# Products of a zero tile on TensorE ahead of and between the first transposes of a hybrid encoder layer

## The chip, the cores and the metric

The kernel runs on one core of a Trainium2 chip. The metric is the device time of one execution in microseconds, taken as the median of several runs. A core has five engines with queues of their own: TensorE (PE, its weight loads PEld), VectorE (DVE), ScalarE (ACT), GpSimd (POOL) and SyncE (SP), which here issues nearly all DMA transfers. Each engine takes its instructions in the order in which they stand; semaphores tie the engines together.

## The reference

One layer of an encoder over 1024 tokens of width 1024, all in float32, with a norm ahead of and behind each part:

```
h = rms_norm(x, g_mix_pre)
aq, ak, av, dqkv, dgate, dalpha, dbeta = split(h @ w_in)
attn_o = window_attention(rope(aq), rope(ak), av, sink)          # 8 heads, +-128 tokens
dn_o   = gated_deltanet(dqkv, dgate, dalpha, dbeta, conv_w, ...) # 4 heads, both directions
x = x + rms_norm(concat(attn_o, dn_o) @ w_out, g_mix_post)
x = x + rms_norm(cross_attention(rms_norm(x), rms_norm(mem)), g_cross_post)  # 256 memory tokens
f = (silu(gate) * up) @ w_down                                   # gate, up = h' @ w_gate_up, 2816 wide each
x = x + rms_norm(f, g_ffn_post)
```

The change concerns only the first line, `h = rms_norm(x, g_mix_pre)`, and the first projections of it.

## The kernel before

The kernel is one long program for one core. Every float32 matrix product is made of three products of a shorter float type: each operand is split into a rounded part (`hi`, a cast on ScalarE, line 103) and what is left (`lo`, a subtraction on VectorE or GpSimd, line 104), and hi·hi, lo·hi and hi·lo are summed in PSUM (`gemm_b`, line 276).

The program has these stages: the norm of x and its transposition; the projections, with convolutions and the chunked products of the DeltaNet (to about 350 us); the scan over eight chunks in both directions, interleaved with the windowed attention and the projections of the memory (to about 545 us); then the output projection, cross-attention and the feed-forward part, in a form with fewer products.

At the start, x is loaded as eight token tiles `xt` of 128 x 1024, in two halves of four (lines 211 to 216). With them come `grow`, the gain as rows, and `ident`, the identity for transpositions. For each half, ScalarE sums the squares of a token tile (line 230) and takes a root (168), VectorE inverts it (169) and scales the tile in place (233). TensorE then transposes 128 x 128 pieces of the four tiles (239), four pieces to a PSUM tile `ps`, of which there are five. ScalarE casts such a tile times the gain to `hhi` (241), VectorE cuts the rest to `hlo` (242). The first projections (276) use them as they come:

```
for k in range(KT):
    pt = small()
    for j in range(4):
        nc.tensor.transpose(pt[:, j * P:(j + 1) * P], xts[4 * hf + j][:, k * P:(k + 1) * P], ident)
    g = gcol[:, k:k + 1]
    cast = nc.scalar.activation(hi[:, k, :], pt, AF.Identity, scale=g)
    cut = nc.vector.scalar_tensor_tensor(lo[:, k, :], pt, g, f32(hi[:, k, :]), ALU.mult, ALU.subtract)
```

The order on each engine isn't the order of the code. A scheduler places the instructions by its own timeline of the whole program, with raised priority for weight loads and some orders pinned by `issue_after`. So an instruction that is added at the start can change what stands where further on.

The names of the scan that the prediction uses: `kv` holds a chunk's keys, values and queries, `psc` are the scan's PSUM tiles (line 843); VectorE corrects `kv` (871) before TensorE can go on. In the attention, `sc` are scores and probabilities, scaled by VectorE at line 703; `ptw` their transposes (711), `ph` and `pl` their split, and `pow` their products with the values (716). The weights of the memory's keys are split by ScalarE (`whi`) and GpSimd (`wlo`). The DeltaNet's products of keys and queries, in float32 without a split, are at line 474.

The pool `wt` has one buffer under the tag `A`, which is used next for `abT` near 47 us; the pool `pg` has three PSUM tiles of 512 columns, used in turn by the projections.

Of the kernel before, what the change touches and what calls it, by code (L numbers as in the profile page):

```python
# [10 lines left out]
F32 = mybir.dt.float32  # L11
# [8 lines left out]
P = 128  # L20
# [56 lines left out]
def tile_hybrid_block(  # L77
# [6 lines left out]
    nc = tc.nc  # L84
# [4 lines left out]
    if dump is None:  # L89
        def dump(name, ap):  # L90
            pass


    def f32(ap):
        return ap.bitcast(F32)
# [12 lines left out]
    def pool(name, bufs, **kw):  # L108
        return tc.tile_pool(name=name, bufs=bufs, reuse_waits="tile", **kw)
# [41 lines left out]
    wt = p1.enter_context(pool("wt", 1, side="right"))  # L151
# [15 lines left out]
    def inverse_root(rs, ss, scale, bias):  # L167
        root = nc.scalar.activation(rs, ss, AF.Sqrt, bias=bias, scale=scale)
        nc.vector.reciprocal(rs, rs)
        return root  # L170
# [27 lines left out]
    pg = pgs.enter_context(pool("pg", 3, space=PSUM))  # L198
# [5 lines left out]
    def small():  # L204
        return ps.tile([P, 512], F32, tag="ps", name="ps")


    xts = [t1.tile([P, D], F32, tag="xt", name="xt", bufs=NT) for _ in range(NT)]
# [3 lines left out]
    for t in range(NT):  # L212
        xload.append(nc.sync.dma_start(xts[t], x[t * P:(t + 1) * P, :]))
        if t == 0:
            nc.sync.dma_start(grow, g_mix_pre[0].rearrange("(c p) -> c p", p=P))
            nc.sync.dma_start(ident, consts[:, 0:P])
    warm = t1.tile([P, 1], F32, tag="ss", name="warm", bufs=4)
    nc.scalar.activation(warm, epsc, AF.Sqrt)
    pt = small()
# [3 lines left out]
    for hf in range(2):  # L223
        hi = hx.tile([P, KT, HALF], F32R, name=f"hhi{hf}")
        lo = hx.tile([P, KT, HALF], F32R, name=f"hlo{hf}")
        for j in range(4):
            xt = xts[4 * hf + j]
            junk = t1.tile([P, D], F32, tag="junk", name="junk", bufs=1)
            ss = t1.tile([P, 1], F32, tag="ss", name="ss", bufs=4)
            nc.scalar.activation(junk, xt, AF.Square, accum_out=ss)  # L230
            rs = t1.tile([P, 1], F32, tag="rs", name="rs", bufs=4)
            rooted = inverse_root(rs, ss, 1.0 / D, epsc)
            scaled = nc.vector.tensor_scalar(xt, xt, rs, None, ALU.mult)
        if hf == 0:
            ready.append((rooted, scaled))
# [6 lines that stand above are left out]
            cut = nc.vector.scalar_tensor_tensor(lo[:, k, :], pt, g, f32(hi[:, k, :]), ALU.mult, ALU.subtract)  # L242
            if hf == 0 and k == 5:
                ready.append((cast, cut))
        hT.append((hi, lo))
        dump(f"hT{hf}", (hi, lo))

# [82 lines left out]
    for hf in range(2):  # L330
        pp = pg.tile([P, 512], F32, tag="pg", name="pg")
        for k in range(KT):
            for a in range(2):
                nc.tensor.matmul(pp, wabr[:, k, :], hT[hf][a][:, k, :], start=(k == 0 and a == 0),
                                 stop=(k == KT - 1 and a == 1))
# [693 lines left out]
    pg = p3.enter_context(pool("pg3", 4, space=PSUM))  # L1029
# [335 lines left out]
    def four(spec):  # L1365
        return [p_.tile([P, HALF], F32, tag=t_, name="pst") for p_, t_ in spec]
# [8 lines left out]
    A = four([PG] * 4)  # L1375
# [155 lines left out]
    for e in range(EARLY):  # L1531
        f = 2 * e
        w, A = [], []
# [84 lines left out]
    pg = L0.enter_context(pool("pg4", 8, space=PSUM))  # L1618

    def bank(name):  # L1620
        return pg.tile([P, 512], F32, tag="pg", name=name)

    for f in (2 * p for p in turns):
# [10 lines left out]
        for i, (W1, W22, (S1, S2, S3, S4), *_) in enumerate(wts):  # L1634
            a1, v, u = (tg.tile([P, 512], F32, tag=n, name=n, bufs=b_) for n, b_ in (("a1", 1), ("v", 2), ("u", 1)))
            A = None
            if early:
                nc.sync.dma_start(a1, d_m1[f + i])
            else:
                A = bank("pA")  # L1640
# [10 lines left out]
        for i, (W1, W22, (S1, S2, S3, S4), *_) in enumerate(wts):  # L1651
            A, D_, E_, v = st[i]
# [105 lines left out]
    A = [bank("pdA") for _ in range(4)]  # L1758
# [118 lines left out]
```

## Time and profile before

| | |
|---|---|
| median of 3 runs | 1521.06 us (1518.25 to 1524.97) |
| profiled execution | 1518.84 us, its span 1516.8 us |
| TensorE busy | 1471.5 us, 97% of the span |
| VectorE, ScalarE, GpSimd busy | 1101.3, 784.2, 362.8 us |
| DMA | 256.34 MB, mean 169 GB/s |

In the profile a row of the order of time has the start and the length in us, then the engine, the line of the code, the operation, the tile written and the tiles read, sizes, and a count where like instructions are merged. Brackets hold the idle time of the engine just before, and what ended it. A row of windows has for each engine the busy time and the number of instructions, and behind these the granted clock of TensorE as a share of full speed, the DMA's busy share and GB/s. Matmuls are pipelined, so that the length of one is longer than the step from one to the next.

### The profile page before, as it was taken

To read this page: it belongs to the slowest core of one execution; us is meant where nothing else is said; L and a number is where in the kernel's file an instruction comes from. 1 tells how busy PE (TensorE), PEld (TensorE's weight loads), DVE (VectorE), ACT (ScalarE), POOL (GpSimd) and SP (SyncE) were. 2 spreads that over 40 slices of the span, in tenths; PEclk is the share of its full clock that TensorE was granted. 3 is DMA by queue.
4 is the path that set the end of the run, shared out by engine and by line. 5 is a ranking of instruction groups with operands and counts; after the bars stand their busy time and mean duration, and the time that the engine had idled before them with its cause. 6 is when DMAs were issued, how large, how long until landed. Compare 5 with 4: busy or idle time off the path is not lost.

```text
span 1516.8 us, 21323 instructions
## 1 busy us (share of the span) xinstructions
PE 1471.5 (97%) x7437; PEld 1239.2 (82%) x7437; DVE 1101.3 (73%) x1801; ACT 784.2 (52%) x1606; POOL 362.8 (24%) x394
## 2 busy tenths in 40 slices
PE   7999999998999999999999998999999999999998
PEld 6888877888989878887788876888888888888787
DVE  5878998676998775538466867776867764696666
ACT  7678844567556764555454684332332332453533
POOL 0011232432325303342201002433524342000030
PEclk9999999999999999999999999999999999999999
DMA  6245554557987584448625553334434333853255
GB/s 203 70 118 142 148 164 129 157 171 193 345 283 234 180 293 158 162 151 262 232 90 180 194 190 123 118 119 132 132 112 152 126 103 116 323 207 97 105 179 168
DMA packets 257751, 256.34 MB, mean 169 GB/s; under 512 B 18128, under 2 KB 190317, under 8 KB 257645
## 3 DMA queue, kind: packets, MB, share of 16 engines
q1 hardware_dynamic: 256493, 252.90, 52.3%
q10 hardware_dynamic: 1152, 2.10, 0.4%
q8 instruction: 58, 0.95, 0.3%
q14 instruction: 48, 0.39, 0.1%
HBM read 178.63 MB, written 73.70 MB: 166 GB/s over the span
## 4 chain that ended last, share of the span: by engine, by line
PE 64%; DVE 8%; DMA 5%; ACT 2%; issue 2%; POOL 1%; SPq 0%; DVEq 0%; ACTq 0%; POOLq 0%
PE pE L1514 8%; PE pD L1514 8%; PE pA L1514 6%; PE pmg L1104 6%; PE pdX L1720 6%; PE pst L1320 5%; PE pdA L1720 4%; PE pB L1514 4%; PE pcq L276 3%; PE psc L843 2%; PE pdD L1720 2%; DMA wpart<-in_w_co_dram 1%; PE pg L276 1%; DMA kv<-d_kv 1%; PE pcv L999 1%
## 5 line engine op out<-in xcount | busy, mean ns | idle before, releaser
L103 ACT CAST whi<-wraw 128x1024 fp32r<-128x1024 f32 x96 | 100.8, 1050 | 120.3 <-DMA wraw<-in_w_gate_up_dram 38.7
L276 PE MATMUL pg<-hlo,whi 128*128 128x512 f32 x352 | 140.0, 398 | 0.0
L276 PE MATMUL pg<-hhi,whi 128*128 128x512 f32 x352 | 139.4, 396 | 0.0
L276 PE MATMUL pg<-hhi,wlo 128*128 128x512 f32 x352 | 139.0, 395 | 0.0
L104 POOL TENSOR_TENSOR wlo<-wraw,whi 128x1024 fp32r<-128x1024 f32 x36 | 87.8, 2441 | 186.4 <-ACT whi L103 182.8
L1514 PE MATMUL pA<-b,whi 128*128 128x512 f32 x352 | 109.8, 393 | 3.6 <-ACT m L1541 2.8
L104 DVE TENSOR_TENSOR wlo<-wraw,whi 128x1024 fp32r<-128x1024 f32 x60 | 74.7, 1245 | 42.2 <-ACT whi L103 38.2
L1514 PEld LDWEIGHTS pA<-b,whi 128*128 128x128 f32 x352 | 65.2, 188 | 18.7 <-ACT m L1541 4.1
L1720 PE MATMUL pdX<-dhl,whi 128*128 128x512 f32 x264 | 76.1, 390 | 1.5 <-ACT dhl L103 0.8
L276 PEld LDWEIGHTS pg<-hhi,whi 128*128 128x128 f32 x352 | 66.5, 189 | 13.4 <-ACT hhi L241 0.3
L276 PEld LDWEIGHTS pg<-hlo,whi 128*128 128x128 f32 x352 | 66.5, 189 | 12.5
L276 PEld LDWEIGHTS pg<-hhi,wlo 128*128 128x128 f32 x352 | 66.5, 189 | 12.5
L1597 POOL TENSOR_TENSOR act<-act,up 128x512 f32<-128x512 f32 x33 | 51.0, 1546 | 82.0 <-DVE up L1596 60.9
L103 ACT CAST whi<-araw 128x1024 fp32r<-128x1024 f32 (+1 forms) x36 | 35.3, 981 | 67.1 <-PE pdX L1720 27.6
L1514 PE MATMUL pA<-b,wlo 128*128 128x512 f32 x176 | 68.8, 392 | 0.5 <-DVE wlo L104 0.5
L104 DVE TENSOR_TENSOR wlo<-araw,whi 128x1024 fp32r<-128x1024 f32 (+1 forms) x36 | 40.7, 1131 | 36.2 <-ACT whi L103 36.1
L1569 POOL TENSOR_TENSOR sr<-wraw 128x512 f32<-128x512 f32 x22 | 29.9, 1359 | 150.6 <-DMA wraw<-in_w_gate_up_dram 88.6
L301 DVE SCALAR_TENSOR_TENSOR acc<-cp,cols,acc 128x1024 f32<-128x1024 f32 x48 | 63.0, 1314 | 0.2
L1720 PEld LDWEIGHTS pdX<-dhl,whi 128*128 128x128 f32 x264 | 49.3, 188 | 12.7 <-ACT dhl L103 1.1
L103 ACT CAST dhl<-b 128x512 fp32r<-128x512 f32 x66 | 40.4, 620 | 31.9 <-PE pdA L1720 13.6
L1514 PE MATMUL pB<-s0h,s1h 128*128 128x512 f32 x176 | 54.4, 390 | 0.7 <-ACT s1h L103 0.7
L103 ACT CAST s0h<-sr 128x512 fp32r<-128x512 f32 x22 | 13.7, 622 | 78.7 <-POOL sr L1569 78.2
(503 smaller groups left out, 4306.1 us busy)
## 6 DMA issues: line engine op xcount, KB each, us to landing
wraw<-in_w_gate_up_dram SPq DMA_DIRECT2D x54, 512.0 KB, 3.8
kv<-d_kv SPq DMA_DIRECT2D x32, 512.0 KB, 7.2
wraw<-in_w_in_dram SPq DMA_DIRECT2D x22, 512.0 KB, 4.0
b<-in_w_down_dram SPq DMA_DIRECT2D x20, 512.0 KB, 6.3
araw<-d_as SPq DMA_DIRECT2D x20, 512.0 KB, 3.6
pz<-d_pz SPq DMA_DIRECT2D x32, 256.0 KB, 6.6
wraw<-in_w_ckv_dram SPq DMA_DIRECT2D x16, 512.0 KB, 4.7
wraw<-in_w_out_dram SPq DMA_DIRECT2D x16, 512.0 KB, 4.5
```

Source lines behind the costliest of these rows:

```text
L103: nc.scalar.copy(hi, src)
L104: return (eng or nc.vector).tensor_tensor(lo, src, f32(hi), ALU.subtract)
L276: nc.tensor.matmul(p_, w[:, k, :], ah[a][:, k, :], start=(k == 0 and i == 0), stop=(k == nk - 1 and i == 2))
L301: nc.vector.scalar_tensor_tensor(acc, cp[:, t:t + S], taps[t], acc, ALU.mult, ALU.add)
L843: nc.tensor.matmul(out[:, d, h, :], lt[:, d, h, :], rt[:, d, h, :], start=True, stop=True)
L999: nc.tensor.matmul(pp[t], mT[a][:, k, t * P:(t + 1) * P], w[:, kk, :], start=(k == 0 and i == 0), stop=(k == KT - 1 and i == 2))
L1104: nc.tensor.matmul(pp[t], act[a][:, k, tt], w_[:, kk, :], start=(k == 0 and i == 0), stop=(k == KT - 1 and i == 2))
L1320: nc.tensor.matmul(bank, a[:, tt], w, start=(start and i == 0), stop=(stop and i == 2), skip_group_check=not check)
L1514: nc.tensor.matmul(out_, w[a][:, k, :], xx[b_][:, k, :], start=(start and k == 0 and i == 0), stop=(k == HK - 1 and i == 2), skip_group_ch ...
L1569: nc.gpsimd.tensor_tensor(s[0], b_[:, 0:HK], b_[:, HK:], ALU.add)
L1597: nc.gpsimd.tensor_tensor(o_, o_, up, ALU.mult)
L1720: nc.tensor.matmul(banks[t], a[:, k - k0, tt], w, start=(first and k == 0 and i == 0), stop=(k == NB - 1 and i == 2), skip_group_check=not ...
```

## The change

A tile of zeros, `still` (128 x 128), is cleared by GpSimd. `idle_turns(n, moving)` issues n float32 products with `still` as the stationary operand into a PSUM tile `spare`, which nothing reads. Twelve with `still` itself as the moving operand stand ahead of everything else on TensorE. Two each are written behind the first half's transposes with the first 128 columns of the token tiles 0, 1 and 2 as the moving operand, so they wait for the scaling of these tiles. `still` takes the buffer `A` of `wt`, `spare` one of the three of `pg`.

```diff
         if t == 0:
             nc.sync.dma_start(grow, g_mix_pre[0].rearrange("(c p) -> c p", p=P))
             nc.sync.dma_start(ident, consts[:, 0:P])
+    still = wt.tile([P, P], F32, tag="A", name="still")
+    nc.gpsimd.memset(still, 0.0)
+    spare = pg.tile([P, 512], F32, tag="pg", name="spare")
+
+    def idle_turns(n, moving):
+        for _ in range(n):
+            nc.tensor.matmul(spare[:, 0:P], still, moving, start=True, stop=True)
+
+    idle_turns(12, still)
     warm = t1.tile([P, 1], F32, tag="ss", name="warm", bufs=4)
     nc.scalar.activation(warm, epsc, AF.Sqrt)
     pt = small()
...
             if hf == 0 and k == 5:
                 ready.append((cast, cut))
+        if hf == 0:
+            for j in range(3):
+                idle_turns(2, xts[j][:, 0:P])
         hT.append((hi, lo))
```

Nine lines are added ahead of the norm and three behind its first half, so a line of the kernel before stands 9 or 12 lines further down in the changed one: 239 is 248, 276 is 288, 703 is 715, 871 is 883.

On TensorE, the first instructions of the program before (`xt_127` and `xt_128` are the token tiles 0 and 1, the tiles `ps` take the pieces k = 0 to 4):

```order
L220 MATMUL ps_149<-ident_68,grow_135 128x8
L239 MATMUL ps_182<-ident_68,xt_127 128x128
L239 MATMUL ps_189<-ident_68,xt_127 128x128
L239 MATMUL ps_196<-ident_68,xt_127 128x128
L239 MATMUL ps_203<-ident_68,xt_127 128x128
L239 MATMUL ps_210<-ident_68,xt_127 128x128
L239 MATMUL ps_182<-ident_68,xt_128 128x128
```

And in the changed program, at the same place:

```order
L223 MATMUL spare_149<-still_147 128x128 x12
L229 MATMUL ps_164<-ident_68,grow_135 128x8
L248 MATMUL ps_197<-ident_68,xt_127 128x128
L248 MATMUL ps_204<-ident_68,xt_127 128x128
L248 MATMUL ps_211<-ident_68,xt_127 128x128
L248 MATMUL ps_218<-ident_68,xt_127 128x128
L223 MATMUL spare_149<-xt_127,still_147 128x128 x2
L248 MATMUL ps_225<-ident_68,xt_127 128x128
L248 MATMUL ps_197<-ident_68,xt_128 128x128
```

The twelve stand first; two turns stand among the transposes of tile 0, and in the same way two each between those of the tiles 1 and 2 and of 2 and 3. Behind tile 3, the order of the first products and transposes is the same as before: one product, four transposes, three products, and so on.

On VectorE, in the scan near 412 to 420 us of the profile before, where the last window of the first group of heads (`sc` of 256 columns) is scaled and the fourth chunk's `kv` is corrected:

```order
L699 TENSOR_TENSOR es_4015<-es_4015,ssum_3988 128x4
L903 TENSOR_TENSOR of_4743<-psc_4749,EG_582 128x512
L104 TENSOR_TENSOR pl_4031<-ptw_4025,ph_4030 128x512
L700 RECIPROCAL es_4015<-es_4015 128x4
L104 TENSOR_TENSOR pl_4042<-ptw_4036,ph_4041 128x512
L904 TENSOR_TENSOR of_4743<-of_4743,psc_4744 128x512
L703 TENSOR_SCALAR sc_3992<-sc_3992,es_4015 128x256
L703 TENSOR_SCALAR sc_3997<-sc_3997,es_4015 128x256
L703 TENSOR_SCALAR sc_4002<-sc_4002,es_4015 128x256
L703 TENSOR_SCALAR sc_4007<-sc_4007,es_4015 128x256
L871 SCALAR_TENSOR_TENSOR kv_4953<-psc_4958,nEG_628,kv_4953 128x128 x4
```

The same place in the changed program:

```order
L711 TENSOR_TENSOR es_4036<-es_4036,ssum_4009 128x4
L712 RECIPROCAL es_4036<-es_4036 128x4
L104 TENSOR_TENSOR pl_4052<-ptw_4046,ph_4051 128x512
L915 TENSOR_TENSOR of_4764<-psc_4770,EG_603 128x512
L715 TENSOR_SCALAR sc_4013<-sc_4013,es_4036 128x256
L715 TENSOR_SCALAR sc_4018<-sc_4018,es_4036 128x256
L715 TENSOR_SCALAR sc_4023<-sc_4023,es_4036 128x256
L715 TENSOR_SCALAR sc_4028<-sc_4028,es_4036 128x256
L104 TENSOR_TENSOR pl_4063<-ptw_4057,ph_4062 128x512
L916 TENSOR_TENSOR of_4764<-of_4764,psc_4765 128x512
L883 SCALAR_TENSOR_TENSOR kv_4974<-psc_4979,nEG_649,kv_4974 128x128
```

The four scalings of `sc` have moved ahead of one cut (`pl`) and of the addition at line 916; the correction of `kv` still stands behind all of them.

## The prediction

> **What bounds the kernel now.** I read the page first, then the table of windows, then the order of time of the first 30 us, and last the waits of TensorE with the windows around them.
>
> ```profile
> span 1516.8 us, 21323 instructions
> ...
> PE 1471.5 (97%) x7437; PEld 1239.2 (82%) x7437; DVE 1101.3 (73%) x1801; ACT 784.2 (52%) x1606; POOL 362.8 (24%) x394
> ```
>
> TensorE is busy for 1471.5 of 1516.8 us, so 45.3 us of idle time is all there is to take. The windows of 50 us show where it lies (length of the window, then busy time of PE, PEld, DVE, ACT, POOL, then the granted clock).
>
> ```profile
> 0.00:50.00 50.00, 41.55 (x192) 33.70 (x193) 33.34 (x55) 34.99 (x60) 0.82 (x15) 1.00 0.57 175
> 50.00:100.00 50.00, 50.00 (x243) 41.47 (x243) 40.52 (x65) 33.58 (x67) 3.04 (x10) 1.00 0.29 85
> ...
> 350.00:400.00 50.00, 45.44 (x310) 41.22 (x310) 38.40 (x99) 33.09 (x71) 10.93 (x12) 0.97 0.93 279
> 400.00:450.00 50.00, 47.43 (x370) 45.67 (x370) 46.36 (x124) 27.17 (x63) 12.67 (x10) 0.97 0.91 291
> ```
>
> The first 50 us have 8.45 us of idle time; the next, the first of three rows alike, have none. So whatever TensorE gains before about 28 us is still there at 200 us. From 350 to 450 us, in the scan, it idles again and VectorE is nearly as busy as TensorE. The start itself:
>
> ```profile
> 0.90 0.20 POOL L250 MEMSET rows<- 128x128 f32 x1
> ...
> 5.62 0.24 PE L220 MATMUL ps<-ident,grow 8*128 8x8 f32 x1 [5.62 <-DMA ident<-in_consts_dram]
> 6.98 1.33 PE L239 MATMUL ps<-ident,xt 128*128 128x128 f32 x5 [1.12 <-DVE xt L233]
> 9.38 1.33 PE L239 MATMUL ps<-ident,xt 128*128 128x128 f32 x5 [1.08 <-DVE xt L233]
> 11.05 2.70 PE L239 MATMUL ps<-ident,xt 128*128 128x128 f32 x10 [0.34 <-DVE xt L233]
> 12.93 3.00 ACT L241 ACTIVATE hhi<-ps,gcol 128x512 fp32r<-128x512 f32 x5 [0.18 <-PE ps L239]
> 13.67 0.80 PE L276 MATMUL pg<-hhi,whi 128*128 128x512 f32 x1
> 14.73 1.12 PE L239 MATMUL ps<-ident,xt 128*128 128x128 f32 x4 [0.26 <-DVE hlo L242]
> 16.07 0.63 PE L276 MATMUL pg<-hhi,wlo 128*128 128x512 f32 x1
> 16.50 0.63 PE L276 MATMUL pg<-hhi,whi 128*128 128x512 f32 x1
> 18.21 0.55 PE L276 MATMUL pg<-hhi,wlo 128*128 128x512 f32 x1
> 18.59 0.39 PE L276 MATMUL pg<-hhi,whi 128*128 128x512 f32 x1
> 18.82 0.60 PE L239 MATMUL ps<-ident,xt 128*128 128x128 f32 x4
> ...
> 25.41 0.75 DVE L233 TENSOR_SCALAR xt<-xt,rs 128x1024 f32<-128x1024 f32 x1
> 27.84 1.80 PE L239 MATMUL ps<-ident,xt 128*128 128x128 f32 x15
> ```
>
> The clock column says 1.00 here, yet the products say otherwise: from 16.07 to 16.50 is 0.43 us for one 512-wide product, from 18.21 to 18.59 it is 0.38, and from 18.59 to 18.82 only 0.23. Ten transposes take 2.70 us (0.27 each) at 11.05, and fifteen 1.80 (0.12 each) at 27.84. TensorE runs at half speed until about 18.5. When the clock changes can be read later in the same trace, in windows of half a microsecond, and what stood ahead of a change in windows of 3.41 us:
>
> ```profile
> 366.50:367.00 0.50, 0.50 (x5) 0.49 (x4) 0.04 (x1) 0.49 (x3) 0.00 (x0) 0.69 0.91 224
> 370.00:370.50 0.50, 0.50 (x4) 0.37 (x3) 0.50 (x2) 0.00 (x0) 0.00 (x0) 0.90 1.36 245
> 421.00:421.50 0.50, 0.50 (x5) 0.50 (x4) 0.50 (x3) 0.00 (x0) 0.00 (x0) 0.80 1.06 393
> 537.00:537.50 0.50, 0.41 (x3) 0.41 (x4) 0.30 (x4) 0.50 (x2) 0.20 (x1) 0.85 1.02 389
> 533.94:537.35 3.41, 1.56 (x11) 1.01 (x10) 3.20 (x9) 1.18 (x4) 0.20 (x1) 1.00 1.03 401
> 11.73:15.14 3.41, 3.11 (x12) 1.87 (x11) 2.99 (x4) 3.23 (x5) 0.00 (x0) 1.00 1.07 384
> 15.14:18.56 3.42, 3.42 (x13) 2.90 (x12) 2.97 (x6) 3.42 (x8) 0.00 (x0) 1.00 0.98 360
> ```
>
> A mean clock of 0.69 over a half-microsecond that begins at 1.0 and ends at 0.5 puts the fall at 366.69; in the same way the rise behind it is at 370.10, and two other falls are at 421.30 and 537.35. The stay at half speed is 3.41 us, and the falls lie 54.61 and 170.66 us apart, 16 and 50 times 3.413. So the clock is decided on a fixed grid of 3.413 us. Counted back 102 steps from 366.69, the grid has an edge at 18.56, just where the products quicken, and before it at 15.14, 11.73, 8.32 and 4.90. The window from 15.14 to 18.56 was full and lifted the clock; the one from 11.73 to 15.14 was busy for 3.11 of 3.41 us, 91%, and did not. The window ahead of the fall at 537.35 was busy for 1.56 us, 46%. So: nearly full lifts, under half lowers.
>
> **The change part by part.** What the turns cost, and whether such products count for the clock at all:
>
> ```profile
> 365.98 0.46 PE L843 MATMUL psc<-kv,pz 128*128 128x128 f32 x2 [1.84 <-issue]
> 366.76 1.92 PE L843 MATMUL psc<-vg,kv 128*128 128x128 f32 x8
> 420.18 1.27 PE L843 MATMUL psc<-kv,pz 128*128 128x128 f32 x8 [2.41 <-DVE kv L871]
> L474 PE MATMUL ps<-acc 128*128 128x128 f32 x128 | 16.4, 275 | 0.0
> ```
>
> The window from 366.69 to 370.10, which lifted the clock, was filled mostly with 128-wide f32 products, the same shape as the turns: 1.92/8 = 0.24 us each at half speed, and 16.4/128 = 0.13 at full speed (line 474).
>
> *The first twelve turns.* Their tile is cleared by GpSimd where the row at 0.90 stood, so they begin at about 1.15. At 0.24 to 0.27 us they take 2.9 to 3.2 us and end by 4.4, before the 5.62 at which the gain's transposition gets its data. They cost nothing; the cover is the transfer of the identity. But they also fill no window: at most 3.2 of 3.41 us (94%) if the grid fell exactly right, and with an edge at 4.90 about 2.9 (84%). I take it that they do not lift the clock, and that if they did it would fall again at 8.32, since the window from 4.90 to 8.32 would hold about 1.1 us of work at full speed, less than the 1.56 that let it fall at 537.35.
>
> The Trainium skill (TensorE: Matmul & The Clock Gate, Part 1) says that a window of about 3.4 us, running free of the kernel's start, lifts the clock after being busy, and that it returns to half speed after an idle window; read simply, gaps shorter than 3.4 us are harmless. The grid and its length agree with the trace; the second half does not: the clock fell after gaps of 1.84 and 2.41 us. By the page's reading the clock would be up from about 5 us on, a rival below.
>
> *The six turns between the token tiles.* Two stand behind the transposes of each of the tiles 0, 1 and 2. At half speed a tile then takes 7 x 0.27 = 1.89 us instead of 1.33. Tile 0 ends at 8.87, hidden, since tile 1 comes at 9.38. Tile 1 ends at 11.27, tile 2 at 13.16, where 12.40 stood before: tile 3's transposes, ScalarE's first cast (12.93) and the first product (13.67) come 0.75 us later. That is the price if the clock gains nothing. What it buys: TensorE is now busy without a break from 9.38 to about 14.9. A stretch of 5.6 us holds a whole window of 3.41 for (5.6 - 3.41)/3.41 = 64% of the grid's positions, more if 94% is enough. With the edges of this trace the window from 11.73 to 15.14 has a gap of about 0.2 us left, 94%.
>
> *What an earlier rise is worth.* I walk the fixed order of TensorE: one product, four transposes, three products, four transposes, three products, four transposes. Before, the last of these end at 18.82 + 0.36 = 19.18, and from there TensorE runs at full speed. With the clock up from the start and no delay: 13.67, the transposes wait for the cut until 14.73, then 0.48 + 0.69 + 0.48 + 0.69 + 0.48 gives 17.55, a gain of 1.6 us. With the rise at 15.14 and the 0.75 us delay: the transposes start at 15.4 and the last end at 18.2, a gain of 1.0. With no earlier rise: 0.75 us of half-speed work is left over at 18.56, a loss of 0.4, up to 0.75. What is late next is the last token tile, scaled at 25.41 + 0.75 = 26.16; its five transposes are the end of the fifteen at 27.84, so a shift of 1.6 us still fits. I take the middle case, -1.0, between -1.6 and +0.75.
>
> *The order behind it.* The scheduler, given a different start, places about a sixth of TensorE's products differently, up to the end of the scan near 550 us; behind that TensorE's order is the same. The work is the same, so this costs or gains only through waits and falls of the clock. One place shows the size:
>
> ```profile
> 400.92 1.39 DVE L703 TENSOR_SCALAR sc<-sc,es 128x384 f32<-128x384 f32 x4
> 414.46 4.74 POOL L104 TENSOR_TENSOR wlo<-wraw,whi 128x1024 fp32r<-128x1024 f32 x2 [2.75 <-ACT whi L103]
> 414.84 5.02 DVE L703 TENSOR_SCALAR sc<-sc,es 128x256 f32<-128x256 f32 x4
> 200.00:550.00 350.00, 331.67 (x2097) 293.37 (x2096) 276.64 (x648) 213.30 (x509) 117.92 (x187) 0.99 0.69 212
> ```
>
> Four scalings of 384 columns take 1.39 us; four of 256 take 5.02 when GpSimd splits weights at the same time. VectorE loses over 3.6 us, the scan's correction queued behind it is late, TensorE idles for 2.41 us and then loses 3.41/2 = 1.7 us to the half clock: 4.1 us seen on TensorE, 5.3 if VectorE's loss goes through whole. In the new order the four scalings stand two places earlier, ahead of one cut and one addition, so they may run before GpSimd starts, or another set may be caught. In all TensorE idles for 350 - 331.67 = 18.3 us from 200 to 550 us. From both sides one such event is worth -5.3 to +5.3. I take zero for the sum, since the same pieces stand in both orders and nothing says which way.
>
> **The sum.** The profiled execution took 1518.84 us, 2.0 more than its span; 1518.84 - 1.0 = 1517.8. It is 2.2 us under the median of the three runs, so against the median 1521.06 the forecast is 1520.0.
>
> **The rivals.** *The turns do not lift the clock earlier* (zero operands may not count, or 94% may not be enough, as 91% was not): then the change costs 0.4 to 0.75 us and the time is 1521.6. For: the 91% window. Against: the window at 366.69. Chance 0.15.
>
> *The clock is up from 5 us and stays*, since no gap at the start reaches a whole step of the grid: the walk gives -1.6, and 1519.5. (The page of the Trainium skill named above leads to this.) The falls after 1.84 and 2.41 us speak against it. Chance 0.07.
>
> *The new order is worse.* VectorE's scalings meet GpSimd's splits in the scan twice more than before. Each meeting costs up to 5.3 us: 2 x 5.3 - 1.0 = +9.6, or 1530.7. It decides from the second further meeting on; one alone gives 1525.4. For: scalings and splits go on through the whole scan, and a shift of 1 or 2 us can bring a meeting about. Against: of the two sets above only one met a split, and the shift is small. Chance of two or their equal 0.16.
>
> *The new order is better.* The meeting at 414.84 goes (-5.3), and with it one more wait like that at 365.98 (1.84, with 1.7 of half clock behind it): -8.8 - 1.0, or 1511.3. For: the scalings stand earlier now. Against: GpSimd's split moves with the same casts. Chance 0.13.
>
> **How the numbers follow.** The forecast, a gain near 1 us with a reordering worth at most one event either way, has a chance of 0.49; its own range is 1515 to 1525. With the two small rivals 0.71 lies within 0.5% (7.6 us), which is about what a measurement of this kernel can tell from no change; 0.13 is faster, 0.16 slower. The range of 8 in 10 reaches to the two large cases: 1511 to 1530.
>
> **What would show it.** Right: twelve products on TensorE from about 1.2 to 4.4 us, half-speed transposes of tile 2 ending near 13.2, 512-wide products 0.23 us apart from about 15 us on instead of 18.6, the fifteen transposes of the second half about 1 us earlier than 27.84, and no idle time of TensorE from there to 200 us. Wrong in the start: products 0.43 apart until 18.5, or transposes 0.12 apart at 7 us. Wrong in the order: the idle time of TensorE from 200 to 550 us, 18.3 us before, differs by over 5 us, or another number of falls of the clock there than three.

## The result, and the profile after

The changed kernel takes 1525.74 us (median of 20 runs, 1521.91 to 1528.46), the kernel before in the same comparison 1520.95 (20 runs, 1513.90 to 1524.97). The ratio is 1.003, 95% interval 1.0019 to 1.0040: slower by 0.19 to 0.40%, some 3 to 6 us. The forecast was 1520.0, a gain of 1 us. The profiled execution took 1526.91 us, against 1518.84 before. Its page begins so (the columns are those shown of before):

```profile
span 1525.1 us, 21402 instructions
...
PE 1481.6 (97%) x7473; PEld 1248.0 (82%) x7473; DVE 1092.6 (72%) x1801; ACT 780.7 (51%) x1604; POOL 366.4 (24%) x395
```

The span is 8.3 us longer. TensorE's idle time is 43.5 us, 1.8 less than before, and its busy time 10.1 us more. It has 36 more instructions for 18 products, so each product of the change is two of them. The table of windows tells where the idle time now lies:

```profile
100.00:150.00 50.00, 47.45 (x254) 40.28 (x254) 36.25 (x52) 39.66 (x116) 10.93 (x13) 1.00 0.43 117
...
200.00:550.00 350.00, 330.39 (x2076) 292.20 (x2075) 267.81 (x641) 204.92 (x509) 118.53 (x187) 0.98 0.68 208
```

The window from 100 to 150 us, one of the three rows alike that had no idle time, now has 2.55 us of it. From 200 to 550 us there are 19.6 us, 1.3 more than the 18.3 of before: the scan, where the prediction looked for trouble, is not where the time went. Products that stand in both programs say the same. The transposition of `rows`, at 34.5 us before, comes 0.6 us earlier. The first product of the output projection, behind everything that was reordered, comes at 551.9 instead of 543.9 us, 8.0 later. From there to the end only 0.3 us is added. So in these two profiles the loss arises between 34 and 544 us. The two executions lie 8.1 us apart and the medians 4.8, so the account that follows is one of this pair.

The start, in order of time:

```profile
1.15 4.54 PE L223 MATMUL spare<-still 128*128 128x128 f32 x24 [1.15 <-POOL still L218]
7.04 0.66 PE L248 MATMUL ps<-ident,xt 128*128 128x128 f32 x4 [1.20 <-DVE xt L242]
11.32 1.33 PE L248 MATMUL ps<-ident,xt 128*128 128x128 f32 x5 [0.15 <-DVE xt L242]
17.61 0.60 PE L248 MATMUL ps<-ident,xt 128*128 128x128 f32 x4
27.73 1.80 PE L248 MATMUL ps<-ident,xt 128*128 128x128 f32 x15
```

The twelve products are 24 instructions and fill 4.54 us, up to 5.69; the gain's transposition starts at 5.62, as before. They did lift the clock: tile 0's four transposes at 7.04 stand 0.12 us apart. It fell again at 11.35, at tile 2 (five transposes in 1.33 us at 11.32), one step later it was up, and the last four early transposes stand at 17.61; before, they stood at 18.82. A gain of 1.2 us at the start is there; whether the products brought it is asked further on. (The fifteen transposes begin at 27.73, against 27.84, but in the new order five more products stand ahead of them.)

What TensorE waits for at 142.48, followed back through four engines:

```profile
111.10 1.28 ACT L314 ACT_TABLE_LOAD   x1
112.40 1.06 ACT L314 ACTIVATE acc<-acc 128x1024 f32<-128x1024 f32 x1
113.47 1.28 ACT L507 ACT_TABLE_LOAD   x1
114.77 0.60 ACT L507 ACTIVATE E<-ps 128x512 f32<-128x512 f32 x1
115.40 0.69 DVE L525 TENSOR_TENSOR U<-ps,E 128x512 f32<-128x512 f32 x1 [3.42 <-ACT E L507]
116.12 0.36 SPq L526 DMA_DIRECT2D d_u<-U  x1
121.99 1.11 SPq L537 DMA_DIRECT2D d_pz<-pm  x2
124.57 0.69 DVE L536 TENSOR_TENSOR pm<-pc,C 128x512 f32<-128x512 f32 x1 [4.33 <-DMA d_pz<-pm]
128.75 0.57 SPq L561 DMA_DIRECT2D b<-d_beta  x1
133.44 1.22 DVE L565 SCALAR_TENSOR_TENSOR A<-V,b 64x1024 f32<-64x1024 f32 x1 [1.95 <-DMA b<-d_beta]
134.69 3.48 DVE L313 SCALAR_TENSOR_TENSOR acc<-cp,cols,acc 128x1024 f32<-128x1024 f32 x2
138.20 1.06 ACT L314 ACTIVATE acc<-acc 128x1024 f32<-128x1024 f32 x1 [4.66 <-DVE acc L313]
141.16 1.27 ACT L503 ACTIVATE gm<-C,ghi 128x128 fp32r<-128x128 f32 x4
142.48 0.50 PE L504 MATMUL ps<-gm,mU_r 128*128 128x512 f32 x1 [2.55 <-ACT gm L503]
```

And the same instructions in the kernel before (line numbers 12 lower):

```profile
111.71 0.60 ACT L495 ACTIVATE E<-ps 128x512 f32<-128x512 f32 x1
112.33 1.28 ACT L302 ACT_TABLE_LOAD   x1
113.45 0.68 DVE L513 TENSOR_TENSOR U<-ps,E 128x512 f32<-128x512 f32 x1
114.16 0.36 SPq L514 DMA_DIRECT2D d_u<-U  x1
119.27 1.11 SPq L525 DMA_DIRECT2D d_pz<-pm  x2
121.88 0.69 DVE L524 TENSOR_TENSOR pm<-pc,C 128x512 f32<-128x512 f32 x1 [2.17 <-DMA d_pz<-pm]
125.47 0.74 SPq L549 DMA_DIRECT2D b<-d_beta  x1
128.20 1.22 DVE L553 SCALAR_TENSOR_TENSOR A<-V,b 64x1024 f32<-64x1024 f32 x1
134.28 1.06 ACT L302 ACTIVATE acc<-acc 128x1024 f32<-128x1024 f32 x1
```

Read the first lines of each. Before, ScalarE takes the exponential `E` (of the decays, for the next key products) and then the silu of a convolution (`acc`). In the new order the silu stands first, with a table load ahead of it and another behind it, and `E` comes 3.06 us later. VectorE stands still for `E`; the store of `U` leaves 1.96 us later, and with it everything queued behind it on SyncE: the stores of `pm` 2.72, the load of `b` 3.28. VectorE's `pm` waits for the store, its scaling by `b` for the load, with two convolution taps behind it. ScalarE waits for the taps, and TensorE for `gm` behind the silu.

The clock: two windows at the start, one ahead of a fall, and half a microsecond with a fall in it:

```profile
1.11:4.52 3.41, 3.37 (x16) 3.37 (x17) 0.00 (x0) 1.16 (x2) 0.32 (x6) 1.00 0.78 219
4.52:7.93 3.41, 2.21 (x19) 2.00 (x19) 0.99 (x3) 1.93 (x4) 0.00 (x0) 1.00 0.91 279
...
301.49:304.90 3.41, 2.66 (x18) 2.15 (x18) 3.41 (x10) 0.27 (x1) 1.93 (x5) 1.00 0.02 5
376.50:377.00 0.50, 0.50 (x1) 0.22 (x1) 0.50 (x2) 0.50 (x2) 0.00 (x0) 0.58 0.95 302
```

Read as the prediction reads them, the falls are at 304.90 and 376.58, 21 steps of 3.413 us apart. Three more, found in the same way, are at 284.42, 342.45 and 543.83, on the same grid. Before there were three from 100 to 550 us, here five. At 1.7 us each, an estimate from the 3.41 us at half speed, two more falls are 3.4 us. Idle time is 2.6 us more from 75 to 220 us and 1.6 us more from 220 to 550 (rows below). Together that is 7.6 us, of the 8.6 between the two landmarks.

### The profile page after: what moved, and what is told of

The parts are those of the page before. It is cut to its first block, busy times and chain, and to the rows that moved or that the text cites. A ratio compares the mean times of both kernels' runs of the same rounds, so it can differ in the third digit from the quotient of the medians.

```text
span 1525.1 us, 21402 instructions
## 1 busy us (share of the span) xinstructions
PE 1481.6 (97%) x7473; PEld 1248.0 (82%) x7473; DVE 1092.6 (72%) x1801; ACT 780.7 (51%) x1604; POOL 366.4 (24%) x395
## 4 chain that ended last, share of the span: by engine, by line
PE 63%; DVE 7%; DMA 7%; issue 2%; ACT 1%; SPq 1%; POOL 0%; DVEq 0%; ACTq 0%
PE pE L1526 8%; PE pD L1526 8%; PE pA L1526 6%; PE pmg L1116 6%; PE pdX L1732 6%; PE pst L1332 5%; PE pcq L288 4%; PE pB L1526 4%; PE psc L855 3%; PE pdA L1732 2%; PE pdD L1732 2%; PE pco L1231 1%; DMA b<-in_w_down_dram 1%; PE pg L288 1%; PE pdX L1836 1%
## 5 line engine op out<-in xcount | busy, mean ns | idle before, releaser
L1526 PE MATMUL pD<-b,s0h 128*128 128x512 f32 x176 | 54.2, 389 | 0.0
```

The lines of the kernel that those rows point to most:

```text
L1526: nc.tensor.matmul(out_, w[a][:, k, :], xx[b_][:, k, :], start=(start and k == 0 and i == 0), stop=(k == HK - 1 and i == 2), skip_group_ch ...
```

## The experiments

All ratios are to the kernel before, run in the same call. Two theories stood against each other. *The order*: the products themselves cost nothing, but the scheduler's new order does. *The products*: they delay the start, or stand in the way among the transposes.

**Fewer products.** With nine products at the start, the scheduler keeps the order of before (but for the place of one copy on VectorE). With ten, or with two alone behind tile 0, it gives the changed kernel's order, apart from a few instructions. One product more flips it:

```diff
-    idle_turns(12, still)
+    idle_turns(9, still)          # the other kernel: idle_turns(10, still)
...
-            for j in range(3):
-                idle_turns(2, xts[j][:, 0:P])
```

> Nine turns at the head and none between the tiles: the scheduler then keeps the order of the kernel before on every engine, but for one copy of the gain column on VectorE, while the start differs. Theory (the new order costs the time, the turns themselves do not): 0 to 1.5 us faster than before, 1519.5 to 1521. Rival (the turns cost the time, at the start): slower by 3 to 5 us, near 1525.

> Ten turns at the head and none between the tiles: one turn more than nine, but with it the scheduler arrives at the changed kernel's order. Theory (the order costs): slower than before by 4 to 6 us, near 1525.5, like the changed kernel, and 5 us slower than nine turns. Rival (the turns at the start cost): within 0.5 us of nine turns.

> Only two turns, behind tile 0, where they lie in a gap; the scheduler arrives at the changed kernel's order on all engines but for a few instructions. Theory (the order costs): 5 to 6 us slower than before, near 1526, with the clock at the start at half speed until 15 to 22 us. Rival (the turns cost): the same as before within 0.5 us, since almost no turns are left.

> The changed kernel once more on the same chip as the other three. Both theories: 4 to 6 us slower than before. If the start gains 1.2 us as in its first profile, it is 1 us faster than two turns in the same order.

| | products | order | median us | ratio | 95% interval |
|---|---|---|---|---|---|
| nine_turns_old_order | 9 | as before | 1521.04 | 1.0004 | 0.9989 to 1.0018 |
| ten_turns_new_order | 10 | new | 1527.67 | 1.0047 | 1.0031 to 1.0062 |
| two_turns_new_order | 2 | new | 1525.09 | 1.0034 | 1.0020 to 1.0049 |
| changed_again | 18 | new | 1527.86 | 1.0049 | 1.0031 to 1.0068 |

The time goes with the order, not with the number of products. The changed kernel is not 1 us faster than the kernel with two products either, as it would be if a gain at the start reached the end. The mean granted clock of one profile does not sort them: it was 0.988 in the profile of the nine, at ratio 1.0004. Over all executions it is 0.994 before, 0.992 for the nine and 0.988 to 0.992 for the other three, and within a kernel the longer executions tend to have the lower clock.

**Products and order apart.** For the next runs the order was held: at the end of the program's text each engine's instructions are chained one behind the other in a written sequence (an edge of issue order, no wait), so that the scheduler has nothing left to choose. The sequence is that of the kernel before or that of the changed one.

```diff
+        for first, then in zip(chain, chain[1:]):      # chain: one engine's instructions in the held order
+            tc.add_manual_dep(then, first.name, mybir.DependencyInfo(
+                mybir.DependencyClass.NoSync, mybir.DependencyReason.DATA), reason="held")
```

> All eighteen products of the change, at their places; every other instruction of every engine is held in the order that it had in the kernel before. Theory (the new order costs, the turns do not): 1519 to 1522 us, ratio 0.999 to 1.001; the fifteen transposes start about 1 us earlier than before, and the gap of PE for gm near 142 us is not there. Rival (the products themselves cost the time): as the changed kernel, 1525 us or more, ratio 1.003 to 1.005.

> None of the eighteen products; every instruction of every engine is held in the order that the changed kernel has. Theory (the order costs): 1525 to 1528 us, ratio 1.003 to 1.005, with gaps of PE for gm near 142 us and for ph near 375 us, and five or more falls of the granted clock after 100 us. Rival (the products cost): as before, 1519 to 1522 us, ratio about 1.000.

All eighteen products in the old order: 1520.08 us, ratio 0.9997 (0.9981 to 1.0013). No product in the new order: 1526.44 us, ratio 1.0043 (1.0028 to 1.0058). The rival falls: the order accounts for the whole loss, within the scatter, and the products are worth nothing that can be measured. One part of the first expectation failed: TensorE still waits for `gm`, 0.64 us, at 138.65. The waits named for the second are there, 2.55 us for `gm` at 143.69 and 3.90 for `ph` at 376.66, and five falls of the clock behind 100 us. The second half's transposes in the first of the two, and the windows from 75 to 220 and from 220 to 550 us of before, changed, eighteen products in the old order, and none in the new:

```profile
26.48 1.80 PE L248 MATMUL ps<-ident,xt 128*128 128x128 f32 x15
```

```profile
75.00:220.00 145.00, 144.72 (x754) 122.79 (x753) 125.89 (x189) 107.59 (x289) 30.72 (x58) 1.00 0.50 141
220.00:550.00 330.00, 311.94 (x2006) 277.26 (x2005) 257.40 (x617) 205.14 (x492) 107.44 (x167) 0.98 0.71 216
```

```profile
75.00:220.00 145.00, 142.10 (x738) 119.96 (x737) 119.96 (x178) 103.44 (x281) 27.93 (x45) 1.00 0.48 135
220.00:550.00 330.00, 310.39 (x1982) 275.46 (x1980) 249.21 (x616) 199.24 (x490) 113.43 (x180) 0.97 0.69 212
```

```profile
75.00:220.00 145.00, 143.73 (x745) 120.97 (x743) 124.59 (x186) 105.76 (x288) 30.88 (x57) 1.00 0.50 140
```

```profile
75.00:220.00 145.00, 142.45 (x731) 120.67 (x730) 120.83 (x180) 103.49 (x280) 26.73 (x46) 0.99 0.48 133
```

The fifteen transposes at 26.48 instead of 27.84 are the 1 us that the prediction sought, in an order where they are the same fifteen. From 75 to 220 us TensorE idles 0.28 us before, 1.27 with all products in the old order, 2.90 in the changed kernel, 2.55 without a product in the new order. VectorE is busy 126 and 125 us in the old order, 120 and 121 in the new: it gets 5 us less of its work done there.

**Which part of the order.** Two kernels without products take the new order only up to the chunk systems, near 220 us, or only behind them.

> None of the eighteen products. Up to the chunk systems (about 220 us) every engine is held in the changed kernel's order, behind that in the order of the kernel before. Theory (most of the loss arises at one place of the early part, where VectorE waits for the load of b with two convolution taps behind it, ScalarE for the taps and TensorE 2.5 us for gm behind that): 1524 to 1526 us, ratio 1.002 to 1.003, with that wait near 142 us. Rival (the loss comes from the order of the chunk systems, windows and scan): 1520 to 1522 us, ratio at most 1.001.

> None of the eighteen products. Up to the chunk systems (about 220 us) every engine is held in the order of the kernel before, behind that in the changed kernel's order. Theory (loss in the early part): 1521 to 1523 us, ratio 1.000 to 1.0015, no wait for gm near 142 us. Rival (loss in the late part): 1524 to 1527 us, ratio 1.002 to 1.004.

The early part: 1524.28 us, ratio 1.0024 (1.0012 to 1.0036). The late part: 1521.38, ratio 1.0011 (1.0000 to 1.0022). The sum, 0.35%, is near the 0.43% of the whole. By the medians some two thirds of it are early; the late part alone is hardly clear of nothing.

**The links of the chain, one by one.** Two single moves in the changed kernel's held order. The first puts the four `gm` scalings ahead of the silu at 138.20; the second puts the two taps ahead of the scaling by `b` at 133.44:

```diff
 ScalarE:  E, gm x4,
+          gm x4 (141.16),
           silu (138.20), cast, copy, scaling,
-          gm x4 (141.16)
 VectorE:  tap, tap,
-          A by b (133.44),
           tap, tap,
+          A by b (133.44)
```

> The changed kernel with its order held, but for one move on ScalarE: the four decay scalings that TensorE waits for at 142.48 us (L503, 1.27 us) stand ahead of the activation (L314) for which ScalarE sits idle 4.66 us before 138.20, with a cast and two evictions behind it. Theory (the waits that the new order brings add to the time one by one): TensorE's 2.55 us wait near 142 us is gone, and the time is 1522 to 1524 us, 2 to 4 us under the changed kernel's 1525 to 1528. Rival (a wait taken away there comes back later, since TensorE runs into the next tile that is not ready): 1525 to 1528 us as the changed kernel, with the gap turned up elsewhere before 250 us.

> The changed kernel with its order held, but for one move on VectorE: the two convolution taps (L313) that stand behind the scaling of A by b (L565), for which VectorE waits 1.95 us on a load until 133.44, stand ahead of it. Theory (that wait starts the chain VectorE, ScalarE, TensorE that ends in the 2.55 us wait for gm at 142.48): the taps run from 131.5, the silu ScalarE waits for ends near 135 in place of 139.3, TensorE's wait is gone with nothing in its place, and the time is 1522.5 to 1524.5 us, 2 to 4 us under the changed kernel's 1525 to 1528. Rival (the wait comes back later, in the chunk systems, whose start hangs on the same A): 1525 to 1528 us.

`gm` first: 1526.44 us, ratio 1.0046 (1.0031 to 1.0061), no gain. TensorE's wait of 2.55 us is cut to 0.63, but the next two links (the squares behind `gm` on ScalarE, and `pc` on VectorE) bring back 0.54 and 0.64. Taps first: 1524.18 us, ratio 1.0033 (1.0019 to 1.0048). The wait for `gm` is gone:

```profile
133.79 1.06 ACT L314 ACTIVATE acc<-acc 128x1024 f32<-128x1024 f32 x1 [0.62 <-DVE acc L313]
139.39 0.39 PE L504 MATMUL ps<-gm,mU_r 128*128 128x512 f32 x1
```

The silu is 4.4 us earlier and TensorE does not stand still ahead of this product, as expected; at 143.18 it waits 0.69 us for `pc`. Yet a gain in time cannot be told from the scatter, and my theory of that run, that this one wait is the cost, is not borne out. Both moves leave VectorE's idle time at the head of the chain where it was: in both runs VectorE still waits 3.4 us for `E` and 4.3 us for the store of `pm`.

**The head of the chain.** One pair on ScalarE is exchanged near 112 us, nothing else, in three kernels:

```diff
 changed kernel, held (and the one with the new order in its early part):
+  E  (L507)
   silu (L314)
-  E  (L507)
 kernel before, held:
-  E  (L495)
   silu (L302)
+  E  (L495)
```

> The changed kernel with its order held, but for one exchanged pair on ScalarE near 112 us: the exponential E (L507), whose input is there, stands ahead of the silu (L314) and not behind it, as in the kernel before. Theory (this pair starts the chain: VectorE waits 3.42 us for E, the store of U comes later and SyncE's queue with it, then VectorE waits 4.3 us on the store of pm and 1.95 us on the load of b, ScalarE 4.7 us for the taps, TensorE 2.55 us for gm): VectorE's 3.4 us wait for E is gone, its wait on the load of b and TensorE's wait for gm too, and the time is 1522 to 1524 us, ratio 1.001 to 1.0025. Rival (no one pair makes it; VectorE is nearly full from 150 to 250 us in both orders and the loss comes from there): 1525 to 1528 us, ratio 1.003 to 1.005.

> The kernel before with its order held, but for the same pair exchanged the other way: the exponential E (L495) behind the silu (L302). Theory (the pair starts the chain): VectorE waits about 3.4 us for E, SyncE's queue comes later, TensorE waits for gm near 142 us, and the time is 1522.5 to 1525 us, ratio 1.001 to 1.0025. Rival: as before, 1519.5 to 1522 us, ratio about 1.000.

> The kernel with the changed kernel's order in the early part only (ratio 1.0024), with the same pair exchanged: the exponential ahead of the silu. Theory: the gap for gm near 142 us is gone and the time is 1519.5 to 1522 us, ratio at most 1.001. Rival: 1523.5 to 1526 us, ratio 1.002 to 1.003.

| | median us | ratio | 95% interval | without the exchange |
|---|---|---|---|---|
| changed_exp_first | 1523.48 | 1.0019 | 1.0005 to 1.0032 | 1.0030 and 1.0049 |
| before_exp_last | 1526.85 | 1.0037 | 1.0023 to 1.0052 | 1 |
| new_early_part_exp_first | 1522.26 | 0.9997 | 0.9982 to 1.0013 | 1.0024 |

All three medians go as the theory has it, but not equally clearly. The first interval overlaps that of the changed kernel (1.0019 to 1.0040), and the third just touches that of the early part (1.0012 to 1.0036). The second stands clear: the kernel before, with this pair exchanged and no other instruction moved, loses 0.37%, more than expected. (The kernel before in its held order and with nothing else changed was not run; that holding costs nothing is read from 0.9997 with the eighteen products.) In its trace the whole chain stands as in the changed kernel:

```profile
115.80 0.60 ACT L495 ACTIVATE E<-ps 128x512 f32<-128x512 f32 x1
116.42 0.69 DVE L513 TENSOR_TENSOR U<-ps,E 128x512 f32<-128x512 f32 x1 [3.04 <-ACT E L495]
124.92 0.69 DVE L524 TENSOR_TENSOR pm<-pc,C 128x512 f32<-128x512 f32 x1 [4.08 <-DMA d_pz<-pm]
142.04 0.50 PE L492 MATMUL ps<-gm,mU_r 128*128 128x512 f32 x1 [2.29 <-ACT gm L491]
```

And in the changed kernel with the pair put back, TensorE has no wait for `gm`, and from 75 to 220 us it idles 0.32 us, as before the change:

```profile
113.48 0.60 ACT L507 ACTIVATE E<-ps 128x512 f32<-128x512 f32 x1 [1.17 <-PE ps L504]
114.11 0.69 DVE L525 TENSOR_TENSOR U<-ps,E 128x512 f32<-128x512 f32 x1 [0.90 <-ACT E L507]
...
141.00 0.39 PE L504 MATMUL ps<-gm,mU_r 128*128 128x512 f32 x1
75.00:220.00 145.00, 144.68 (x751) 122.47 (x750) 122.10 (x183) 104.77 (x282) 29.41 (x50) 1.00 0.49 137
```

The first row also corrects my expectation: the input of `E` was not there yet. With `E` first, ScalarE stands idle for 1.17 us before it. A scheduler that takes what is ready would take the silu; that this one did so for that reason is not shown.

Here the Trainium skill (ScalarE: Activation LUTs, Table sets: the hidden batching unit) has a rule that speaks for the slower order as a whole: batch activations by table set, since each change of set costs about 2.7 us by the page. Here a load takes 1.28 us and the silu starts right behind it (111.10 and 112.40 above), and the changed program has 32 loads where the program before has 34. The order with fewer loads is the slower one. The exchanged pair itself does not change their number: 34 with `E` behind the silu in the order of before, 32 with `E` ahead of it in the new one. So the number of loads does not explain its price.

**Waits filled with products.** If falls of the clock after waits cost time, products in the waits should save it. In the held order of before, six and eight products of the identity by itself stand ahead of the two scan products that waited 1.84 and 2.41 us (`BEHIND` says behind which place of TensorE's held order they go):

```diff
             pv = bank()
+            n, place = {(1, 0): (6, 1435), (0, 3): (8, 2057)}.get((g, step), (0, 0))
+            for _ in range(n):
+                BEHIND.setdefault(place, []).append(nc.tensor.matmul(pv[:, 0, 0, :], ident, ident, start=True, stop=True).ins)
             mm(pv, pz[:, :, :, 1, :], R)
```

> The kernel before in its own order, with six products of the identity by itself ahead of the product of the scan that waited 1.84 us at 365.98, and eight ahead of the one that waited 2.41 us at 420.18, so that TensorE works through most of both waits. Theory (a fall of the clock after a wait costs its 3.4 us at half speed, 1.7 us of work, beside the wait): the falls at 366.7 and 421.3 are gone, and the time is 1516 to 1518 us, ratio about 0.998. Rival (what is lost at the low clock is waited for anyway, or the falls come elsewhere): 1519.5 to 1522 us, ratio 1.000 or above.

> The kernel before in its own order with the change's eighteen products and with the fourteen products in the two waits of the scan: both parts that came out at or under the time before when alone (0.9997 and 0.9991). If the start's 1 us and the two falls' 3.4 us add up: 1516.5 to 1518.5 us, ratio 0.9975 to 0.9985. Rival (falls come elsewhere as the two are taken away, and the start's gain is waited for): 1519.5 to 1522 us, ratio 0.999 to 1.001.

The first: 1519.14 us, ratio 0.9991 (0.9977 to 1.0005). The falls at 366.7 and 421.3 are gone:

```profile
366.50:367.00 0.50, 0.50 (x5) 0.50 (x5) 0.50 (x1) 0.50 (x3) 0.00 (x0) 1.00 1.09 228
421.00:421.50 0.50, 0.50 (x7) 0.50 (x6) 0.50 (x3) 0.42 (x1) 0.00 (x0) 1.00 1.15 373
```

But others are there instead, at 266.5 and 884.3, and the one near 537 lasts two steps in place of one. The time is not clear of that before, where 0.998 was expected. Both together, the eighteen products and the fills, give 1519.00 us, ratio 0.9987 (0.9974 to 1.0000). That is the lowest ratio of the study, though not to be told from the fills alone. It beats the changed one; that it beats the one before is likely, and not settled.

## Why the prediction was wrong

**The sign was wrong, by one step of the sum: the order behind the start, which I took at zero.** I wrote that nothing said which way it would go, since "the same pieces stand in both orders". The pieces were the same; what stood ahead of what was not, and in the order of ScalarE it could have been read: the exponential that VectorE needs next had gone behind a silu of 1.06 us with a table load on each side of it. I looked for the danger in the scan, at VectorE's scalings and GpSimd's splits near 414 us, because there a large event could be seen in the trace of before. The early part showed no idle time of TensorE before, so I did not search it. But a stretch without idle time has only waits that are hidden, and a new order can uncover them.

**The size of an event was near, by luck.** I gave one event -5.3 to +5.3 us. The exchanged pair alone costs 0.37%, 5.6 us. "One alone gives 1525.4" stood under the rival of the worse order; the time is 1525.74. But the mechanism, scalings that meet splits, is not what happened. The one meeting that I had seen even went away. The durations of the 44 scalings (least, median and most, in ns) before and in the changed kernel, and what TensorE met in the scan instead:

```profile
L703 DVE TENSOR_SCALAR sc<-sc,es x44: 340/415/2430, 295.6 to 542.3; 128x384 f32<-128x384 f32 x32, 128x256 f32<-128x256 f32 x12
```

```profile
L715 DVE TENSOR_SCALAR sc<-sc,es x44: 343/412/562, 300.2 to 551.3; 128x384 f32<-128x384 f32 x32, 128x256 f32<-128x256 f32 x12
376.49 0.74 PE L728 MATMUL pow<-ph,vhl 128*128 128x512 f32 x1 [4.48 <-ACT ph L103]
```

No scaling of the changed kernel takes longer than 0.56 us, and the waits of 1.84 and 2.41 us are gone, as the rival of the better order had it. In their place TensorE waits 4.48 us for `ph`, behind ScalarE (3.89 at 371.59 in the kernel with the late part alone). So TensorE's idle time from 200 to 550 us moved by only 1.3 us. Of my two signs of a wrong order that one stayed silent, and the other, five falls in place of three, showed.

**The start.** The walk gave a gain of 1.0 us for a rise near 15 us; the trace of the changed kernel shows 1.2 us, and with the order held the fifteen transposes come 1.4 us earlier. But that the products bring this gain is not shown. In the trace of old_order_filled_waits, with no product at the start, the last early transposes stand as early, at 17.31, and the fifteen at 26.31:

```profile
17.31 0.60 PE L239 MATMUL ps<-ident,xt 128*128 128x128 f32 x4
```

In changed_exp_first, with all eighteen, they stand at 18.83, as late as before. Where the program starts on the clock's grid differs from run to run (an edge at 4.52 in one profile of the changed kernel, at 6.72 in the other), and single profiles cannot tell this from the products. That the gain survives to 200 us holds in the fixed order up to 139 us, where TensorE waits for `gm`; by 177 us it is used up (1.27 us of idle time between 75 and 220), and in the time it cannot be seen: ratio 0.9997.

**The price of a product was wrong by two.** I took 128 instructions of line 474 for 128 products; they are 64. In the second profile of the changed kernel (changed_again) twelve took 5.49 us, 0.46 each, not 0.24 to 0.27; they end at 5.69 in the one profile and at 6.64 in the other, not by 4.4. There they held up the gain's transposition by 1 us, with no effect, since tile 0 is scaled only by 7.0. Of the six, only the two behind tile 2 ran at half speed: from 11.32 to the start of tile 3 at 13.30 are 1.98 us, near the 1.89 of the prediction by luck: the five transposes took 1.13 where I had 1.35, the two products 0.85 where I had 0.54.

**The first twelve do lift the clock.** I said that they would fill no window. The window from 1.11 to 4.52 us was busy for 3.37 of 3.41 us (row above). That the clock would fall again, since the next windows hold little, was right in kind; it came one step later, at 11.35.

**The falls.** The grid held: the falls of the changed kernel are whole steps of 3.413 us apart. "Under half lowers" was too narrow. The window ahead of the fall at 304.90 was busy for 2.66 of 3.41 us, 78%, while the one from 4.52 to 7.93, busy for 2.21 us, 65%, let the clock stay up. So the busy share of one window does not decide a fall by itself; what does stays open.

**The rival from the page of the Trainium skill on the clock gate** (TensorE: Matmul & The Clock Gate, Part 1), that the clock would be up from 5 us and stay, fell: it was up from 4.52 and fell at 11.35, with gaps of at most 1.7 us.

**What stays open.** The late part of the new order, 0.11%, was not taken apart; the 4.48 us for `ph` are the first place to look. The parts do not add up closely: the pair alone costs 0.37%, the whole early part 0.24%, and the changed kernel with the pair put back still loses 0.19% (0.05 to 0.32). Why the exchanged pair costs 5.6 us when TensorE's idle time up to 220 us grows by only 2.7 is not settled either. In that profile (1525.3 us) the first product of the output projection comes 3.0 us later than before, at 546.9, and the rest arises behind it, where nothing was reordered, with falls at 888.3 and 932.7 that the trace before does not have. Falls move from run to run.

## What to carry to other kernels

When a change makes a scheduler choose anew, compare the orders engine by engine, and ask of each exchanged pair which engine waits for the one that now comes second; price it by the rows of the one that now comes first. Hold the order and test the change alone: of a change of 18 products, all that could be measured came from the order of instructions that it never touched, and one exchanged pair of them is enough for a loss of that size. Look for a wait's cause at the head of its chain: here two moves at its end took the wait away or made it smaller, and no gain in time could be told.

## What the runs showed of the hardware

Products of a tile of zeros count as work for the clock: after twelve of them the first transposes took 0.12 us each, 0.27 before. A float32 product of 128 columns is two instructions on TensorE (24 for twelve products), a float32 transpose of the same size one (five for the five of a tile). The mean granted clock of one profile is no measure of the kernel's time: the profile with nine products had a mean of 0.988 at ratio 1.0004, that with none in the new order 0.994 at 1.0043; over their twelve executions each the two have 0.992 and 0.991. And two falls that were filled away (366.7 and 421.3) came back at two other places.
